# A hybrid S5 and attention layer on one core: TensorE's order written out by hand in the recurrence stage, the gelu in one activation, the skip folded into the kernel matrix

## The chip, the cores and the metric

The kernel runs on one core of one Trainium2 chip. The metric is the device time of one execution in microseconds; the median of several runs is compared. The profile names the engines PE (TensorE, matmuls), PEld (its weight loads), DVE (VectorE), ACT (ScalarE), POOL (GpSimd) and SP (SyncE, which here only issues transfers). Each engine works through its own instructions in a fixed order.

## What is computed

One encoder layer over two requests (1024 and 256 tokens, 1280 in all, model width 1024). After an RMS norm one projection gives eight parts. Branch A is a bidirectional diagonal state-space mixer, branch B differential attention. What the change touches is the mixer's recurrence:

```
bu = einsum('ngpc,lgc->nlgp', B_bar, us)
_, h_f = associative_scan(combine, (a[0], bu[0]))
_, h_b = associative_scan(combine, (a[1], bu[1]), reverse=True)
y = real(C[0] h_f + C[1] h_b)
y = y + d_skip * u
ys = gelu(y)                       # tanh form
ys = ys * sigmoid(ys @ w_glu + b_glu) * silu(zs)
...
ya = rmsnorm(diff_attention(rotary(q), rotary(k), v)) * silu(za)
merged = sigmoid(gs) * (ys @ wb[0]) + sigmoid(ga) * (ya @ wb[1])
out = rmsnorm(x + merged @ w_out)
```

## The kernel before

Everything is float32; large matmuls are made of three products of a high and a low part. Tokens are taken in steps of T = 8: J = 160 columns of eight tokens each (128 for the long request, 32 for the short). There are NG = 32 groups of 16 channels with 64 complex states in two directions.

The stages in order: norm, transposition and v; projections for xs, q and k, beside which a generator (`prep_gen`) computes the recurrence's tables, pair of groups by pair, into DRAM (`wb_d`, `wc_d`, `kt_d`, `tt_d`); the recurrence; attention; GLU, merge and output projection.

Four of the projection's parts (zs, za, gs, ga: 24 tiles of 128 columns) are wanted only at the end. They are the filler: `filler_gen` yields after each step of three matmuls (L637 to L639), eight steps for a chunk of columns, three chunks for a tile, 576 steps in all. A chunk is copied out by ACT (`zo`, L643); a tile's weights are loaded by ACT's queue, cast by ACT (L233) and their low part computed by POOL (L234). `fill(n)` traces n steps. In the kernel before the recurrence holds no fill calls: `fill(F_PRE * KD)` = 176 steps stand ahead of the attention's loops, 288 in them, the rest in the GLU stage. The framework's planner simulates the program and sets each engine's order by its own estimates, so the filler steps land in the recurrence where it finds PE free.

The recurrence goes over eight blocks of NB = 4 groups. For a block PE makes the in-projection `pr`, `pi` (L709, L710; weights `wb`, one buffer; moving operand `U`), DVE multiplies them by the table `tb` (L715 to L718), POOL adds and subtracts (L719, L720) to give `bm`, DVE runs four scans (L727, L728) with the decay `rt` that POOL makes (L703), zeroes borders (L731, L732) and turns the result back by `tb` into `e` (L737 to L742). PE makes the out-projection (L749 to L751) from `e` (weights `wcm`) and from `U` (weights `mt`, read from `kt_d`). DVE adds the skip (L754), ACT squares, DVE scales and multiplies (L759, L760), ACT takes a sigmoid (L761), DVE multiplies (L762): that is the gelu. `e` has one buffer; `tb`, `wcm`, `mt` and `U` have two. All loads go through SP (`U` L672, `mt` L675, `wb` L687, `tb` L688, `wcm` L689), in SP's order.

Of the kernel before, what the change touches and what calls it, by code (L numbers as in the profile page):

```python
# [11 lines left out]
F32 = mybir.dt.float32  # L12
F32R = mybir.dt.float32r
I32 = mybir.dt.int32
AF = mybir.ActivationFunctionType
ALU = mybir.AluOpType
# [12 lines left out]
J = JL + JS  # L29
# [6 lines left out]
LAM_INIT = 0.8 - 0.6 * math.exp(0.0)  # L36
CHUNKS = ((0, 512), (512, 512), (1024, 256))
MAGIC = 12582912.0
F_PRE = 22
F_LONG = (4, 1, 2, 0)  # L40
F_SHORT = (3, 2, 3, 0)
F_CHUNKS = ((0, 432), (432, 424), (856, 424))
# [75 lines left out]
def bc(ap, axis, n):  # L118
    shape = list(ap.shape)
    shape.insert(axis, n)  # L120
    return ap.unsqueeze(axis).broadcast_to(shape)
# [3 lines left out]
def kernel(  # L125
# [6 lines left out]
    V, G, A, PE, SP = nc.vector, nc.gpsimd, nc.scalar, nc.tensor, nc.sync  # L132
# [28 lines left out]
    ident = cp.tile([128, 128], F32, name="ident")  # L161
# [8 lines left out]
    r8 = cp.tile([128, NG], F32, name="r8")  # L170
    dcol = cp.tile([128, NG], F32, name="dcol")
    rmask = cp.tile([128, J], F32, name="rmask")
# [75 lines left out]
    def prep_gen():  # L248
# [18 lines left out]
        ps = tr_bank()  # L267
# [13 lines left out]
        t1, t2 = sc("t1"), sc("t2")  # L281
# [27 lines left out]
        for i, dst in enumerate((Cr, Ci)):  # L309
            ps = tr_bank()  # L310
# [74 lines left out]
        for pb in range(NPB):  # L385
# [8 lines left out]
            for n in range(2):  # L394
                for r in range(2):
                    A.activation(Bm[:, :, r, 32 * n:32 * n + 32], Bb[:, :, 16 * r:16 * r + 32], AF.Copy,
                                 scale=hmask[:, n:n + 1])
# [6 lines left out]
            ps = tr_bank()  # L404
            for r in range(2):
                for g in range(2):
                    o = (r * 2 + g) * 128
# [5 lines left out]
            wc = qq.tile([128, 2, 2, T, GC], F32, tag="wc", name="wc", bufs=2)  # L413
# [11 lines left out]
            ps = tr_bank()  # L425
            for g in range(2):
                o = ps[64 * g:64 * g + 64]
# [6 lines left out]
            kt = qq.tile([128, 144], F32, tag="kt", name="kt", bufs=2)  # L434
            A.copy(kt[:, 16:144], ps[:, 16:144])
            for g in range(2):
                A.copy(kt[64 * g:64 * g + 32, 0:16], ps[64 * g:64 * g + 32, 0:16])
            kv = kt_d[pb // 4]
            for g in range(2):
                gi = 2 * (pb % 4) + g  # L440
# [36 lines left out]
    with ExitStack() as p0:  # L477
# [53 lines left out]
        for i in range(10):  # L531
# [6 lines left out]
            ps = mm_bank()  # L538
# [113 lines left out]
    def fill(steps, ins=None):  # L652
        with after(ins):
            for _ in range(steps):
                next(filler, None)
# [4 lines left out]
    with ExitStack() as p2:  # L660
        sp_ = p2.enter_context(tc.tile_pool(name="s5", bufs=1, reuse_waits="tile"))
        ps_b = p2.enter_context(tc.tile_pool(name="ps_b", bufs=2, space=PSUM, reuse_waits="tile"))
        NB = 4
        NBLK = NG // NB
        U = {}
        M = {}
        Y = {}

        def load_u(q):
            u = sl.tile([128, 8, J], F32, tag="U", name="U", bufs=2)  # L670
            for t in range(T):
                SP.dma_start(u[t * 16:(t + 1) * 16], xs_d[q][t].rearrange("(g c) j -> c g j", c=GC))  # L672
            mt = sl.tile([128, 8, 128], F32, tag="mt", name="mt", bufs=2)
            for t in range(T):
                SP.dma_start(mt[t * 16:(t + 1) * 16],  # L675
                             kt_d[q][:, :, (7 - t) * 16:(7 - t) * 16 + 128].rearrange("g c w -> c g w"))
            M[q] = mt
            U[q] = u

        def load_blk(b):  # L680
            tb = sl.tile([128, 2, NB, J], F32, tag="tb", name="tb", bufs=2)
            wb = sl.tile([128, 2, NB, 128], F32, tag="wb", name="wb")
            wc = sl.tile([128, 2, NB, 128], F32, tag="wcm", name="wcm", bufs=2)
            for h in range(2):
                pb = 2 * b + h
                gsl = slice(2 * h, 2 * h + 2)
                SP.dma_start(wb[:, :, gsl], wb_d[pb])  # L687
                SP.dma_start(tb[:, :, gsl], tt_d[pb])  # L688
                SP.dma_start(wc[:, :, gsl], wc_d[pb])  # L689
            return tb, wb, wc  # L690

        load_u(0)
        blk = load_blk(0)
        for b in range(NBLK):
            q, gb = b // 2, (b % 2) * NB
            if b % 2 == 0:
                Y[q] = nrm.tile([128, 8, J], F32, tag="A", name="Y")
                if q + 1 < 4:
                    load_u(q + 1)
            tb, wb, wc = blk  # L700
            u, y, mt = U[q], Y[q], M[q]
            rt = sp_.tile([128, NB, J], F32, tag="rt", name="rt")
            G.tensor_tensor(rt, bc(rmask, 1, NB), bc(r8[:, b * NB:(b + 1) * NB], 2, J), op=ALU.mult)  # L703
            bm = sp_.tile([128, 2, NB, J], F32, tag="bm", name="bm", bufs=2)
            for h in range(NB // 2):
                pr_ = ps_b.tile([128, 2, J], F32, tag="pr", name="pr")
                pi_ = ps_b.tile([128, 2, J], F32, tag="pi", name="pi")
                for g in range(2):
                    PE.matmul(pr_[:, g], wb[:, 0, 2 * h + g], u[:, gb + 2 * h + g], start=True, stop=True)  # L709
                    PE.matmul(pi_[:, g], wb[:, 1, 2 * h + g], u[:, gb + 2 * h + g], start=True, stop=True)  # L710
                t1 = sp_.tile([128, 2, J], F32, tag="t1", name="t1")
                t2 = sp_.tile([128, 2, J], F32, tag="t2", name="t2")
                gsl = slice(2 * h, 2 * h + 2)
                tr_, ti_ = tb[:, 0, gsl], tb[:, 1, gsl]
                V.tensor_tensor(bm[:, 0, gsl], pr_, tr_, op=ALU.mult)  # L715
                V.tensor_tensor(t2, pr_, ti_, op=ALU.mult)
                V.tensor_tensor(t1, pi_, ti_, op=ALU.mult)
                V.tensor_tensor(bm[:, 1, gsl], pi_, tr_, op=ALU.mult)  # L718
                G.tensor_tensor(bm[:, 0, gsl], bm[:, 0, gsl], t1, op=ALU.add)  # L719
                G.tensor_tensor(bm[:, 1, gsl], bm[:, 1, gsl], t2, op=ALU.subtract)  # L720
            n = NB * J
            z = []
            for r in range(2):
                zz = sp_.tile([128, n + 2], F32, tag=f"z{r}", name=f"z{r}")
                rf = rt.rearrange("p g j -> p (g j)")
                bf = bm[:, r].rearrange("p g j -> p (g j)")
                V.tensor_tensor_scan(zz[0:64, 2:n + 2], rf[0:64], bf[0:64], 0.0, ALU.mult, ALU.add)  # L727
                V.tensor_tensor_scan(zz[64:128, 0:n][:, ::-1], rf[64:128, ::-1], bf[64:128, ::-1], 0.0,  # L728
                                     ALU.mult, ALU.add)
                zv = zz[:, 1:n + 1].rearrange("p (g j) -> p g j", j=J)  # L730
                V.memset(zv[0:64, :, 0:J:JL], 0.0)  # L731
                V.memset(zv[64:128, :, JL - 1:J:JS], 0.0)  # L732
                z.append(zv)
            e = sp_.tile([128, 2, NB, J], F32, tag="e", name="e")
            f1 = sp_.tile([128, NB, J], F32, tag="f1", name="f1")
            f2 = sp_.tile([128, NB, J], F32, tag="f2", name="f2")
            V.tensor_tensor(e[:, 0], z[0], tb[:, 0], op=ALU.mult)  # L737
            V.tensor_tensor(f1, z[1], tb[:, 1], op=ALU.mult)
            V.tensor_tensor(e[:, 0], e[:, 0], f1, op=ALU.subtract)
            V.tensor_tensor(e[:, 1], z[1], tb[:, 0], op=ALU.mult)  # L740
            V.tensor_tensor(f2, z[0], tb[:, 1], op=ALU.mult)
            V.tensor_tensor(e[:, 1], e[:, 1], f2, op=ALU.add)  # L742
            if b + 1 < NBLK:
                blk = load_blk(b + 1)
            for h in range(NB // 2):
                py = tr_bank()[:, :2 * J].rearrange("p (g j) -> p g j", j=J)
                for g in range(2):
                    gg = 2 * h + g
                    PE.matmul(py[:, g], wc[:, 0, gg], e[:, 0, gg], start=True, stop=False)  # L749
                    PE.matmul(py[:, g], wc[:, 1, gg], e[:, 1, gg], start=False, stop=False)  # L750
                    PE.matmul(py[:, g], mt[:, gb + gg], u[:, gb + gg], start=False, stop=True)  # L751
                for g in range(2):
                    gg = 2 * h + g
                    V.scalar_tensor_tensor(y[:, gb + gg], u[:, gb + gg], dcol[:, b * NB + gg:b * NB + gg + 1],  # L754
                                           py[:, g], op0=ALU.mult, op1=ALU.add)
            g1 = nrm.tile([128, NB, J], F32, tag="B", name="g1")
            yb = y[:, gb:gb + NB]
            A.activation(g1, yb, AF.Square)
            V.tensor_scalar(g1, g1, 0.044715, 1.0, op0=ALU.mult, op1=ALU.add)  # L759
            V.tensor_tensor(g1, g1, yb, op=ALU.mult)  # L760
            sig = A.activation(g1, g1, AF.Sigmoid, scale=2.0 * math.sqrt(2.0 / math.pi))  # L761
            V.tensor_tensor(yb, yb, g1, op=ALU.mult)  # L762
            if b % 2 == 1:
                for t in range(T):
                    SP.dma_start(gy_d[q][t].rearrange("(g c) j -> c g j", c=GC), y[t * 16:(t + 1) * 16])

    with tc.issue_after(sig.ins):
        tables = A.preload_act_table_set("natural_log_exp_and_others")
# [381 lines left out]
```

## Time and profile before

| what | value |
|---|---|
| median of 3 runs | 1159.61 us (1158.87 to 1161.73) |
| profiled execution | 1156.2 us, its span 1154.0 us |
| granted TensorE clock, mean | 0.982 |
| busy: PE, DVE, ACT, POOL | 94%, 71%, 40%, 34% |

The span runs from the first to the last instruction; the execution's own time has a little around it. Matmuls overlap, so PE's busy time counts stretches in which any is under way, and the distance between two starts is what a matmul costs. The granted clock is a share of full speed.

### The profile page before, as it was taken

The numbers are of one execution on the slowest core, as the hardware profiler recorded it, in microseconds if no ns is written. First come the engines' busy times: TensorE is split into PE (matmuls) and PEld (weight loads), VectorE is DVE, ScalarE is ACT, GpSimd is POOL, SyncE is SP. The second block draws the span as 40 slices with busy tenths as digits, with TensorE's granted clock in tenths as the row PEclk, the third lists the DMA queues.
The fourth block names the chain that finished last, engine by engine and source line by source line (L and its number), as shares of the span: only waits on it lengthen the run. The fifth ranks groups of instructions, "written<-read, shape, count | busy, mean of one in ns | idle before, by whom it ended". The sixth has DMA issues, their size and how long they took to land.

```text
span 1154.0 us, 18198 instructions
## 1 busy us (share of the span) xinstructions
PE 1086.1 (94%) x6539; PEld 998.3 (87%) x6539; DVE 817.4 (71%) x1482; ACT 457.0 (40%) x911; POOL 396.9 (34%) x559
## 2 busy tenths in 40 slices
PE   5999999999989788889999999999999999999997
PEld 5887788778888787779998999889999999998997
DVE  5857968987549999977687687597353575666524
ACT  4443332132211111155565565465364454554322
POOL 1499989831134334212122122121133002520032
PEclk9998999999999888999999999999999999999999
DMA  7834453554475666661641733531455985469222
GB/s 225 228 102 151 144 176 113 184 187 139 158 201 188 149 163 174 174 158 57 158 126 49 197 96 89 152 96 43 124 177 175 283 243 140 136 177 283 70 56 93
DMA packets 193786, 174.13 MB, mean 151 GB/s; under 512 B 33568, under 2 KB 166688, under 8 KB 193696
## 3 DMA queue, kind: packets, MB, share of 16 engines
q1 hardware_dynamic: 158368, 144.65, 43.6%
q10 hardware_dynamic: 35328, 28.32, 7.7%
q8 instruction: 52, 0.85, 0.3%
q14 instruction: 38, 0.31, 0.1%
HBM read 114.23 MB, written 58.69 MB: 150 GB/s over the span
## 4 chain that ended last, share of the span: by engine, by line
PE 51%; DVE 20%; DMA 11%; POOL 8%; issue 6%; ACT 3%; SPq 2%; POOLq 0%; DVEq 0%; ACTq 0%
PE mm L637 6%; PE mm L638 6%; PE mm L639 6%; PE mm L240 3%; PE mm L241 3%; PE mm L242 3%; PE tr L1090 2%; DVE mx L827 2%; PE tr L1092 2%; PE tr L1091 2%; PE S L823 2%; DMA wqs<-in_w_out_dram 2%; DMA wst<-in_w_in_dram 2%; PE S L825 2%; PE tr L848 2%
## 5 line engine op out<-in xcount | busy, mean ns | idle before, releaser
L637 PE MATMUL mm<-hTh,wh 128*128 128x424 f32 (+1 forms) x576 | 210.1, 365 | 1.6 <-ACT zo L643 1.6
L639 PE MATMUL mm<-hTh,wl 128*128 128x424 f32 (+1 forms) x576 | 206.2, 358 | 0.0
L638 PE MATMUL mm<-hTl,wh 128*128 128x424 f32 (+1 forms) x576 | 206.0, 358 | 0.0
L838 POOL TENSOR_SCALAR p<-p,rs 128x1024 f32<-128x1024 f32 (+1 forms) x40 | 41.3, 1034 | 234.0 <-DVE rs L836 154.9
L637 PEld LDWEIGHTS mm<-hTh,wh 128*128 128x128 f32 x576 | 108.6, 189 | 6.6 <-ACT zo L643 2.4
L638 PEld LDWEIGHTS mm<-hTl,wh 128*128 128x128 f32 x576 | 108.8, 189 | 4.3 <-issue 0.2
L639 PEld LDWEIGHTS mm<-hTh,wl 128*128 128x128 f32 x576 | 108.8, 189 | 3.2
L827 DVE TENSOR_REDUCE mx<-S 128x1 f32<-128x1024 f32 (+1 forms) x80 | 84.3, 1058 | 36.9 <-PE S L825 36.1
L240 PE MATMUL mm<-hTh,wh 128*128 128x512 f32 (+1 forms) x288 | 105.8, 367 | 3.6 <-DVE m L604 1.8
L241 PE MATMUL mm<-hTl,wh 128*128 128x512 f32 (+1 forms) x288 | 104.4, 362 | 0.0
L242 PE MATMUL mm<-hTh,wl 128*128 128x512 f32 (+1 forms) x288 | 103.6, 360 | 0.0
L234 POOL TENSOR_TENSOR wl<-wst,wh 128x1024 fp32r<-128x1024 f32 x24 | 62.1, 2588 | 114.0 <-ACT wh L233 114.0
L831 ACT ACTIVATE p<-S,mx 128x1024 f32<-128x1024 f32 (+1 forms) x80 | 79.2, 992 | 53.8 <-DVE mx L828 53.2
L1090 PE MATMUL tr<-wqh,mh 128*128 128x256 f32 x320 | 89.8, 281 | 1.9 <-DVE o L1094 1.8
L1091 PE MATMUL tr<-wql,mh 128*128 128x256 f32 x320 | 89.2, 279 | 0.0
L1092 PE MATMUL tr<-wqh,ml 128*128 128x256 f32 x320 | 89.0, 279 | 0.0
L240 PEld LDWEIGHTS mm<-hTh,wh 128*128 128x128 f32 x288 | 54.7, 190 | 14.5 <-ACT xo L571 2.3
L1097 POOL TENSOR_TENSOR o<-o,finB 128x256 f32<-128x256 f32 x30 | 28.7, 960 | 102.5 <-ACT jk L1096 102.5
L1090 PEld LDWEIGHTS tr<-wqh,mh 128*128 128x128 f32 x320 | 60.1, 188 | 2.9 <-DVE o L1094 2.9
L241 PEld LDWEIGHTS mm<-hTl,wh 128*128 128x128 f32 x288 | 54.7, 190 | 9.2 <-issue 1.4
L242 PEld LDWEIGHTS mm<-hTh,wl 128*128 128x128 f32 x288 | 54.7, 190 | 8.3
L1091 PEld LDWEIGHTS tr<-wql,mh 128*128 128x128 f32 x320 | 60.2, 188 | 0.0
(397 smaller groups left out, 2888.7 us busy)
## 6 DMA issues: line engine op xcount, KB each, us to landing
wst<-in_w_in_dram ACTq DMA_DIRECT2D x24, 512.0 KB, 4.3
wst<-in_w_in_dram SPq DMA_DIRECT2D x16, 512.0 KB, 5.8
wst<-in_w_branch_dram SPq DMA_DIRECT2D x32, 256.0 KB, 4.5
wqs<-in_w_out_dram SPq DMA_DIRECT2D x16, 512.0 KB, 4.4
tt_d<-tt SPq DMA_DIRECT2D x16, 320.0 KB, 2.2
tb<-tt_d SPq DMA_DIRECT2D x16, 320.0 KB, 5.0
zt<-gs_d SPq DMA_DIRECT2D x16, 320.0 KB, 4.2
x<-in_x_sample_dram SPq DMA_DIRECT2D x8, 512.0 KB, 5.3
```

The source lines that it names most:

```text
L234: e.tensor_tensor(l, st, h, op=ALU.subtract)
L240: PE.matmul(ps[:, :n], wh[:, k, :], hTh[:, k, c0:c0 + n], start=(k == 0), stop=False)
L241: PE.matmul(ps[:, :n], wh[:, k, :], hTl[:, k, c0:c0 + n], start=False, stop=False)
L242: PE.matmul(ps[:, :n], wl[:, k, :], hTh[:, k, c0:c0 + n], start=False, stop=(k == KD - 1))
L637: PE.matmul(ps[:, :n], wh[:, k, :], hTh[:, k, c0:c0 + n], start=(k == 0), stop=False)
L638: PE.matmul(ps[:, :n], wh[:, k, :], hTl[:, k, c0:c0 + n], start=False, stop=False)
L639: PE.matmul(ps[:, :n], wl[:, k, :], hTh[:, k, c0:c0 + n], start=False, stop=(k == KD - 1))
L827: V.tensor_reduce(mx, S[:, :nk], axis=AX.X, op=ALU.max)
L831: A.activation(p[:, :nk], S[:, :nk], AF.Exp, bias=mx, scale=1.0 / math.sqrt(HD), accum_out=sm[:, t:t + 1])
L1090: PE.matmul(ps[:, :256], mh[:, k, ts_], oh_[:, k], start=(k == 0), stop=False)
L1091: PE.matmul(ps[:, :256], mh[:, k, ts_], ol_[:, k], start=False, stop=False)
L1092: PE.matmul(ps[:, :256], ml[:, k, ts_], oh_[:, k], start=False, stop=(k == 7))
```

## The change

- In the recurrence stage PE's instructions keep the order in which they are written (`tc.manual_schedule`). That order is: `fill(36)`, in-projection of block 0, and then for each block b the in-projection of block b + 1, `fill(13)`, the out-projection of b, `fill(4)`. That is 172 filler steps; the 176 ahead of the attention go (`F_PRE = 0`).
- The loop is cut into `in_mm`, `scan` and `out_mm`. Block b + 1's `wb`, `tb`, `wcm` are requested before the next `U`, and `mt` is loaded by a function of its own after them.
- `e` has two buffers.
- `rt` is made by four ACT copies of 160 columns with a scale instead of one POOL multiply of 640.
- The gelu is one ACT activation (`Gelu_apprx_tanh`) straight from PSUM, two groups at a time.
- The skip is added to the diagonal of the lag-0 block of `kt` during preparation (two small DVE instructions a pair of groups, in place of two ACT copies), so that the product of `mt` and `U` contains it.
- Two of DVE's four multiplies of the in-projection change places.

```diff
-F_PRE = 22
+F_PRE = 0
+S_PRE, S_MID, S_END = 36, 13, 4
...
             for g in range(2):
-                A.copy(kt[64 * g:64 * g + 32, 0:16], ps[64 * g:64 * g + 32, 0:16])
+                o = slice(64 * g, 64 * g + 16)
+                V.scalar_tensor_tensor(kt[o, 0:16], ident[o, 64 * g:64 * g + 16], dcol[o, 2 * pb + g:2 * pb + g + 1],
+                                       ps[o, 0:16], op0=ALU.mult, op1=ALU.add)
...
+        def load_m(q):
             mt = sl.tile([128, 8, 128], F32, tag="mt", name="mt", bufs=2)
...
-            G.tensor_tensor(rt, bc(rmask, 1, NB), bc(r8[:, b * NB:(b + 1) * NB], 2, J), op=ALU.mult)
+            for g in range(NB):
+                A.activation(rt[:, g], rmask, AF.Copy, scale=r8[:, b * NB + g:b * NB + g + 1])
...
                 V.tensor_tensor(bm[:, 0, gsl], pr_, tr_, op=ALU.mult)
+                V.tensor_tensor(t1, pi_, ti_, op=ALU.mult)
                 V.tensor_tensor(t2, pr_, ti_, op=ALU.mult)
-                V.tensor_tensor(t1, pi_, ti_, op=ALU.mult)
...
-            e = sp_.tile([128, 2, NB, J], F32, tag="e", name="e")
+            e = sp_.tile([128, 2, NB, J], F32, tag="e", name="e", bufs=2)
...
-                for g in range(2):
-                    gg = 2 * h + g
-                    V.scalar_tensor_tensor(y[:, gb + gg], u[:, gb + gg], dcol[:, b * NB + gg:b * NB + gg + 1],
-                                           py[:, g], op0=ALU.mult, op1=ALU.add)
-            g1 = nrm.tile([128, NB, J], F32, tag="B", name="g1")
-            yb = y[:, gb:gb + NB]
-            A.activation(g1, yb, AF.Square)
-            V.tensor_scalar(g1, g1, 0.044715, 1.0, op0=ALU.mult, op1=ALU.add)
-            V.tensor_tensor(g1, g1, yb, op=ALU.mult)
-            sig = A.activation(g1, g1, AF.Sigmoid, scale=2.0 * math.sqrt(2.0 / math.pi))
-            V.tensor_tensor(yb, yb, g1, op=ALU.mult)
+                act = A.activation(y[:, gb + 2 * h:gb + 2 * h + 2], py, AF.Gelu_apprx_tanh)
...
+        load_u(0)
+        blks = {0: load_blk(0)}
+        load_m(0)
+        with tc.manual_schedule(engines={mybir.EngineType.PE}):
+            fill(S_PRE)
+            cur = in_mm(0, blks[0])
+            for b in range(NBLK):
+                if b + 1 < NBLK:
+                    blks[b + 1] = load_blk(b + 1)
+                if b % 2 == 0 and b // 2 + 1 < 4:
+                    load_u(b // 2 + 1)
+                    load_m(b // 2 + 1)
+                e = scan(b, blks[b], *cur)
+                if b + 1 < NBLK:
+                    cur = in_mm(b + 1, blks[b + 1])
+                fill(S_MID)
+                sig = out_mm(b, blks.pop(b), e)
+                fill(S_END)
```

## Rows read from the trace of the kernel before

**Rows 1.** The page: busy time and share of the span of each engine.

```profile
PE 1086.1 (94%) x6539; PEld 998.3 (87%) x6539; DVE 817.4 (71%) x1482; ACT 457.0 (40%) x911; POOL 396.9 (34%) x559
```

**Rows 2.** Windows, recurrence and attention: us, busy of each engine, clock, DMA.

```profile
331.00:503.00 172.00, 142.80 (x748) 134.33 (x747) 163.95 (x234) 27.13 (x41) 60.32 (x45) 0.91 0.64 173
503.00:820.00 317.00, 311.94 (x1840) 289.67 (x1839) 233.76 (x428) 177.26 (x356) 70.44 (x52) 1.00 0.36 104
```

**Rows 3.** Waits of PE, 331 to 503 us: total, times, longest.

```profile
PE tr L749 <- DVE e L739: 8.8, 4, 5.3
PE pr L709 <- DMA wb<-wb_d: 8.7, 3, 4.4
PE tr L749 <- DVE Y L754: 8.3, 3, 4.7
```

**Rows 4.** Timeline of PE: start, duration, instruction.

```profile
304.31 0.36 PE L637 MATMUL mm<-hTh,wh 128*128 128x432 f32 x1
...
306.05 0.36 PE L637 MATMUL mm<-hTh,wh 128*128 128x432 f32 x1
...
348.51 0.56 PE L637 MATMUL mm<-hTh,wh 128*128 128x424 f32 x1
...
357.13 0.43 PE L750 MATMUL tr<-e,wcm 128*128 128x160 f32 x2
...
359.84 0.43 PE L709 MATMUL pr<-U,wb 128*128 128x160 f32 x2
```

**Rows 5.** Groups by line, PE, 304 to 503 us: count, busy, mean, idle before.

```profile
L637 PE MATMUL mm<-hTh,wh 128*128 128x424 f32 (+1 forms) x183 | 66.4, 363 | 1.6 <-ACT zo L643 1.6
```

**Rows 6.** Groups by line, DVE, 332 to 492.6 us (until the last e).

```profile
L754 DVE SCALAR_TENSOR_TENSOR Y<-U,dcol,tr 128x160 f32<-128x160 f32 x25 | 8.1, 374 | 0.4 <-DMA gy_d<-Y 0.3
L762 DVE TENSOR_TENSOR Y<-Y,g 128x640 f32<-128x640 f32 x6 | 7.2, 1199 | 0.1
L759 DVE TENSOR_SCALAR g<-g 128x640 f32<-128x640 f32 x6 | 5.8, 972 | 0.0
L760 DVE TENSOR_TENSOR g<-g,Y 128x640 f32<-128x640 f32 x6 | 5.5, 916 | 0.1
```

**Rows 7.** Timeline of DVE: first multiply, an rt's neighbours, last e.

```profile
332.10 0.49 DVE L715 TENSOR_TENSOR bm<-pr,tb 128x320 f32<-128x320 f32 x1 [22.07 <-PE pr L709]
...
346.07 1.53 DVE L737 TENSOR_TENSOR e<-z,tb 128x640 f32<-128x640 f32 x1
347.53 0.81 DVE L741 TENSOR_TENSOR f<-z,tb 128x640 f32<-128x640 f32 x1
...
491.86 0.81 DVE L742 TENSOR_TENSOR e<-e,f 128x640 f32<-128x640 f32 x1
```

**Rows 8.** Groups by line, POOL, 304 to 503 us.

```profile
L234 POOL TENSOR_TENSOR wl<-wst,wh 128x1024 fp32r<-128x1024 f32 x8 | 23.2, 2902 | 44.9 <-ACT wh L233 44.9
...
L703 POOL TENSOR_TENSOR rt<-rmask,r 128x640 f32<-128x640 f32 x8 | 10.0, 1255 | 35.7 <-DVE z L731 23.3 <-DVE z L732 6.3 <-DVE z L728 3.7
```

**Rows 9.** Timeline of SP's queue: transfers issued, start and time to issue.

```profile
318.17 4.10 SPq L675 DMA_DIRECT2D mt<-kt_d  x8
...
324.23 0.62 SPq L687 DMA_DIRECT2D wb<-wb_d  x1
...
408.73 1.19 SPq L689 DMA_DIRECT2D wcm<-wc_d  x2
...
411.33 1.29 SPq L687 DMA_DIRECT2D wb<-wb_d  x2
```

**Rows 10.** DMA issues, 320 to 352 us: count, size, median us to landing.

```profile
wb<-wb_d SPq DMA_DIRECT2D x4, 256.0 KB, 5.6
```

**Rows 11.** Groups by line, ACT, 304 to 503 us.

```profile
L758 ACT ACTIVATE g<-Y 128x640 f32<-128x640 f32 x8 | 5.9, 739 | 58.4 <-DVE Y L754 58.4
```

**Rows 12.** A one-column DVE instruction (attention), and the busiest window of preparation.

```profile
L828 DVE TENSOR_SCALAR mx<-mx 128x1 f32<-128x1 f32 x79 | 11.4, 145 | 0.4
...
200.00:250.00 50.00, 46.85 (x250) 36.89 (x249) 47.31 (x85) 10.58 (x31) 32.76 (x46) 1.00 0.56 185
```

More of the change, by code (lines that the diff above doesn't have):

```diff
@@ L672, in load_u @@
                 SP.dma_start(u[t * 16:(t + 1) * 16], xs_d[q][t].rearrange("(g c) j -> c g j", c=GC))
+            U[q] = u
+        def load_m(q):
             mt = sl.tile([128, 8, 128], F32, tag="mt", name="mt", bufs=2)
@@ L677, in load_u @@
             M[q] = mt
-            U[q] = u
         def load_blk(b):
@@ L690, in load_blk, with in_mm @@
             return tb, wb, wc
-        load_u(0)
-        blk = load_blk(0)
-        for b in range(NBLK):
+        def in_mm(b, blk):
             q, gb = b // 2, (b % 2) * NB
[L696 to L699, printed above, removed]
             tb, wb, wc = blk
-            u, y, mt = U[q], Y[q], M[q]
+            u = U[q]
             rt = sp_.tile([128, NB, J], F32, tag="rt", name="rt")
-            G.tensor_tensor(rt, bc(rmask, 1, NB), bc(r8[:, b * NB:(b + 1) * NB], 2, J), op=ALU.mult)
+            for g in range(NB):
+                A.activation(rt[:, g], rmask, AF.Copy, scale=r8[:, b * NB + g:b * NB + g + 1])
             bm = sp_.tile([128, 2, NB, J], F32, tag="bm", name="bm", bufs=2)
@@ L720, with scan @@
                 G.tensor_tensor(bm[:, 1, gsl], bm[:, 1, gsl], t2, op=ALU.subtract)
+            return rt, bm
+        def scan(b, blk, rt, bm):
+            tb = blk[0]
             n = NB * J
@@ L742, with out_mm @@
             V.tensor_tensor(e[:, 1], e[:, 1], f2, op=ALU.add)
-            if b + 1 < NBLK:
-                blk = load_blk(b + 1)
+            return e
+        def out_mm(b, blk, e):
+            q, gb = b // 2, (b % 2) * NB
+            wc = blk[2]
+            u, mt = U[q], M[q]
+            if b % 2 == 0:
+                Y[q] = nrm.tile([128, 8, J], F32, tag="A", name="Y")
+            y = Y[q]
             for h in range(NB // 2):
@@ L765 @@
                     SP.dma_start(gy_d[q][t].rearrange("(g c) j -> c g j", c=GC), y[t * 16:(t + 1) * 16])
+            return act
+        load_u(0)
[16 more added lines that the diff above has]
+                fill(S_END)
     with tc.issue_after(sig.ins):
```

## The prediction, on record before the changed kernel was run

> **What bounds the kernel now.** I read the busy shares first. TensorE (PE) is busy 94% of the span [rows 1], so only time in which PE idles or runs at its lower clock can be won. The windows by stage say where that is [rows 2]: in the attention (503 to 820 us) PE is busy 312 of 317 us at clock 1.00, so little is lost there. The recurrence (331 to 503) has PE at 143 of 172 us and a granted clock of 0.91, while VectorE (DVE) is busy 164 of 172.
>
> PE's waits in that stage name DVE twice, 8.8 us for e and 8.3 us for Y, and a load of wb for 8.7 us [rows 3]. So the stage goes at DVE's pace.
>
> How much PE loses there: in the filler (gate projection) nine matmuls start within 1.74 us, 0.193 us each [rows 4], so a step of three is 0.58 us. Twenty passes of the recurrence's matmuls fill 357.13 to 359.84, 0.1355 us each, and its in-projection, 16 passes, takes 2.2 us a block; the 24 passes of the out-projection make 3.25 us, together 43.4 us in eight blocks. From 304 to 503 PE started 183 steps [rows 5], 106.1 us. With 43.4, about 2 us of leftover preparation matmuls, and 1.9 us of eight score matmuls it had 153.4 us of work in 199: **45.6 us are lost**. That is all that the change can win in this stage.
>
> **The change, part by part.**
>
> *DVE loses four kinds of work.* Y's multiply-add (skip), the gelu's scalar step and its two multiplies go: 8.1, 5.8, 5.5 and 7.2 us of the time until the last e [rows 6], 26.6 us in 43 instructions. Consecutive ones overlap by 0.07 us (an instruction that begins at 346.07 and lasts 1.53 ends at 347.60, and the next begins at 347.53 [rows 7]), so 26.6 - 3.0 = 23.6, say 24 us. DVE works from 332.10 to 492.67, 160.5 us, almost without a gap.
>
> *rt leaves POOL for ScalarE.* Eight instructions, 10.0 us of POOL [rows 8]. Where one meets an e multiply, at 346.07, that lasts 1.53 instead of 0.81 us [rows 7]; over the seven inside the stage the stretches add to 3.7 us, 1.7 of them on instructions that go anyway. I count 2 us. The Trainium skill, SBUF — State Buffer, Who interferes with whom, says that a DVE instruction with two SBUF inputs and a GpSimd one that reads SBUF shut each other out for a whole instruction; taken for every rt that would be 10 us, and the sum below 8 us lower. The row at 346.07 agrees with the shutting out, but most rts here meet a DVE instruction with an input in PSUM or none.
>
> *What comes back.* The removed scalar step averages 0.97 us and the last multiply 1.20 [rows 6], against about 0.5 and 0.8 undisturbed: part of their time was POOL's weight split (eight of 2.9 us [rows 8]) or its bm adds standing in the way, and these will now meet other instructions. I give back 3 us. DVE then needs 160.5 - 24 - 2 + 3 = **137.5 us** from first multiply to last e. Bounds: below, the undisturbed times of what stays (eight multiplies at 0.40, four scans at 1.5, memsets 0.45, six e instructions at 0.74 make 14.1 a block, 112.5 in all); above, another 1 us a block for the wait on POOL's last bm add, which gelu work used to cover: 145.5.
>
> *The start.* SP issues U, then eight mt loads for 4.1 us, then block 0's tables, the second half of wb at 324.23 [rows 9]. With mt behind, that half issues at about 320.1 and, with 0.6 us to issue and 5.6 to land [rows 10], is there at 326.3. In the hand order PE has 36 steps first: 304.3 + 20.9 + 2 of preparation = 327.2. So the in-projection starts at 327.2 instead of 331.1 and DVE at about 328. mt is due at the first out-projection, some 15 us later; its loads hide behind the first scans.
>
> *The second block.* There is one wb buffer, so block 1's wb issues when in-projection 0 is over (329.4); its second half is fourth on SP (1.9 us) and lands at 336.9. PE, in order, idles 7.5 us there. DVE is at block 0's scans and does not notice; PE later catches up.
>
> *The end of the stage.* Last e at 328 + 137.5 = 465.5, out-projection 3.3 more: about 469, against 498. PE by then has done 36 + 8 x 13 + 7 x 4 = 168 steps, 97.4 us, with 43.4 and 2 us: 142.8 of 165 us. Lost: 22.2. The steps that were not done here run later, on a PE that has no idle time there; they are inside the balance. **Gain 45.6 - 22.2 = 23.4 us.**
>
> *The second e tile* lets e of a block be written while PE still reads the one before; DVE never waited for it, so nothing is counted. *Gelu in one activation*: two of 320 columns in place of two of 640 at 0.74 us [rows 11]; ScalarE (busy 27 of 172 us) has room for them and for rt's 32 copies (between 0.3 and 0.7 us each, 10 to 22 us).
>
> *The skip in the preparation.* 32 small DVE instructions (16 x 16, out of PSUM) take the place of ScalarE copies. Nearest rows: 0.145 us for one column, 0.374 for the same operation on 160 [rows 6, 12]; 16 columns lie near the first, so 5 us of DVE (bounds 4.6 and 12). DVE is at 47 of 50 us in the tightest part of that stage [rows 12] but has 10 to 30% free elsewhere. I charge 3 us, bounds 0 and 9.
>
> **Sum.** The profiled execution took 1156.2 us: 1156.2 - 23.4 + 3 = 1135.8. The median of the runs is 3.4 us above it, so **1139 us**.
>
> **Rivals.**
>
> *PE's own order sets the pace.* From 339 us (in-projection 1 done) the hand order needs 7.5 + 3.25 + 2.3 + 2.2 = 15.25 us a block: six such, then 13.05 and 10.75, ends at 454.3. That needs DVE to do its part in 123 us, within its bounds but only if most POOL stretches vanish. Lost 7.5, gain 38.1, and with 3 for the preparation 1124 us. For it: PE's stretch is arithmetic. Against: in all windows POOL's wl and bm do stretch DVE.
>
> *rt gives back all of its time.* If each of the eight rts held DVE up for its whole 1.25 us, DVE's part is 8 us shorter, 129.5, and the time 1131 us. For it: the row at 346.07; against: the six others, most of which cost DVE under 1 us. This is what the SBUF page named above would make of it.
>
> *ScalarE becomes the wait.* rt must be ready before each scan, and queues behind zo copies and gelus that wait for PE. If it stands behind the previous gelu: 3.25 us of out-projection, the gelu, 1.5 us of copies, less the 3.2 us of multiplies that run meanwhile, over 2 us a block: stage end near 484, 1154 us.
>
> *The wb load holds up PE (slower).* With one wb buffer and one SP queue the order of issues decides. In the trace wcm goes out at 408.73 and wb only at 411.33 [rows 9], tb between them, and wcm's buffer has to wait for an out-projection. Here that would be four issues ahead of wb and two of its own, 3.7 us, and landing 4.1, against 2.3 us of filler: a stall of 5.5 us a block, and some 1.7 more because PE comes back slow (after the wait for wb that ends at 346 a filler matmul takes 0.56 us, not 0.36 [rows 4], and it goes on like that for 4 us). Six blocks: 43 us on the 454.3, lost 50.7, time 1156.2 + 5.1 + 3 + 3.4 = 1168 us. It decides from 5.9 us a block upward. Against: wb comes free at the in-projection, well before wcm, and SP's order in most blocks had wb first.
>
> **Chances.** DVE's pace as summed 0.50; rt's whole time 0.10; PE's order 0.20; ScalarE 0.07; nothing left after a dearer preparation 0.04; wb 0.09. A difference under 0.3% cannot be told from none here. Faster 0.86, same 0.05, slower 0.09. The range goes from PE's order with a free preparation (1121) to the upper bounds of DVE (gain 15.4) and preparation (9): 1156.2 - 15.4 + 9 + 3.4 = 1153, and the ScalarE case beside it: 1120 to 1154.
>
> **What would show it.** In the changed profile: first bm multiply near 328; last e near 465; DVE busy above 90% between; PE's wait for e in most blocks, under 2 us each; a gap of some 7 us ahead of the second in-projection; clock above 0.95. A wait of DVE for rt, or PE waiting for wb in every block, would say that a rival holds. The number fails most easily in DVE's 137.5 us, whose stretches by POOL depend on who meets whom, and in later stages, if an order there shifts.

## The result, and the profile after

The changed kernel takes 1165.05 us (median of 9 runs, 1161.31 to 1169.93) against 1159.53 us for the kernel before (9 runs beside it): a ratio of 1.0055 [1.0039, 1.0071], 0.6% slower. 1139 was forecast. Its profiled execution took 1166.0 us, its span 1164.2, 10.2 more than before.

Where the 10.2 us come from, by three marks that both traces have (the start of the last matmul of the last out-projection, the start of the last transposition of an attention unit, the end of the span):

| stretch | before | after | difference | of it moved filler steps | left |
|---|---|---|---|---|---|
| start to last out-projection | 498.2 | 479.9 | -18.3 | -8 steps, -4.6 | -13.7 |
| to last transposition (attention) | 324.6 | 348.1 | +23.5 | +4 steps, +2.3 | +21.2 |
| to the end (GLU, merge, output) | 331.2 | 336.2 | +5.0 | +4 steps, +2.3 | +2.7 |

So the recurrence gained, though less than the forecast 20.4 us (23.4 less the 3 charged for the preparation, which lies in the same stretch), and the attention, in whose code the diff changes nothing, lost more. The page's first line (answers to [rows 1]) and the windows of recurrence and attention (us, busy of PE, PEld, DVE, ACT, POOL with instructions, clock, DMA share, GB/s; answer to [rows 2]):

```profile
PE 1082.7 (93%) x6539; PEld 997.9 (86%) x6539; DVE 783.6 (67%) x1458; ACT 456.6 (39%) x911; POOL 377.9 (32%) x551
```

```profile
327.00:480.00 153.00, 126.53 (x713) 123.61 (x712) 128.87 (x176) 30.70 (x67) 43.45 (x38) 0.91 0.69 185
480.00:828.20 348.20, 330.09 (x1896) 305.64 (x1895) 236.96 (x429) 178.11 (x359) 71.07 (x53) 0.98 0.35 101
```

The recurrence still has PE idle for 26.5 of 153 us at the clock of before, 0.91. In the attention, where PE had idled 5 of 317 us at clock 1.00, it now idles 18 of 348 at 0.98.

PE's waits up to the last out-projection (answer to [rows 3]; total, times, longest):

```profile
PE pr L709 <- DMA wb<-wb_d: 11.1, 1, 11.1
PE pr L709 <- DVE z L735: 9.4, 1, 9.4
PE pr L709 <- DVE e L746: 6.0, 1, 6.0
```

All three stand ahead of an in-projection, and by SP's queue all three are waits for `wb`. Two rows name DVE, as what ended last before PE went on; but an in-projection reads no z and no e, and `wb` was issued only at 332.26 and 432.34, and takes 3.0 to 6.6 us to land in this stage. The first of the three in time is the gap forecast ahead of the second block (PE's timeline: start, duration, instruction, idle before):

```profile
328.17 0.43 PE L710 MATMUL pi<-U,wb 128*128 128x160 f32 x2
338.00 0.87 PE L709 MATMUL pr<-U,wb 128*128 128x160 f32 x2 [9.40 <-DVE z L735]
```

The longest is seen on SP's queue (start, time to issue; answer to [rows 9]). The one buffer of `wb` was free when the in-projection before ended, at 373.2, and the program requests `wb` before the next `U`. But SP's order is the planner's, and in it `wb` goes out behind `tb`, which had to wait for block 2's e, behind `wcm`, and then behind 13 us of stores and loads; the last 3 us before it SP waited. The same happens again at 432.34.

```profile
375.17 1.17 SPq L693 DMA_DIRECT2D tb<-tt_d  x2
376.44 1.22 SPq L694 DMA_DIRECT2D wcm<-wc_d  x2
377.76 4.97 SPq L766 DMA_DIRECT2D gy_d<-Y  x8
382.83 3.79 SPq L675 DMA_DIRECT2D U<-xs_d  x8
386.67 4.32 SPq L681 DMA_DIRECT2D mt<-kt_d  x8
394.10 1.18 SPq L692 DMA_DIRECT2D wb<-wb_d  x2
```

DVE, for its part, now waits for PE. Its waits from 327 us, and its first multiply and last e (answer to [rows 7]):

```profile
DVE bm L715 <- PE pr L709: 25.9, 6, 15.9
DVE z L731 <- POOL bm L719: 2.4, 8, 0.3
```

```profile
327.28 0.49 DVE L715 TENSOR_TENSOR bm<-pr,tb 128x320 f32<-128x320 f32 x1 [15.88 <-PE pr L709]
...
472.08 0.82 DVE L746 TENSOR_TENSOR e<-e,f 128x640 f32<-128x640 f32 x1
```

The 15.9 us lie before the first multiply; 10.0 are in the stage. The last out-projection starts 3.9 us after that e has ended (476.82 against 472.90): PE, behind by then, still had the 17 steps that the written order puts between the last two out-projections, 9.8 us.

The attention's new idle time, PE's waits from 480 us on:

```profile
PE tr L869 <- ACT sqh L892: 7.1, 4, 3.1
PE S L844 <- ACT p L852: 3.2, 3, 2.7
PE S L844 <- DMA gs_d<-zo: 1.9, 1, 1.9
PE mm L640 <- ACT zo L646: 1.7, 2, 1.2
PE tr L869 <- DVE mx L849: 1.6, 2, 1.1
```

Four of the five name ACT or DVE, which are busy only 51% and 68% of the stretch: they had the time, but not at that place of their order. Not all of the loss is idle time: between the two marks PE's busy time grew too, from 319.5 to 330.0 us, 2.3 of it for the four steps, at a clock of 0.98 in place of 1.00.

### The profile page after: what moved, and what is told of

Same layout as the page of the kernel before. It is cut to its first block, busy times and chain, and to the rows that moved or that the text cites. A ratio compares the mean times of both kernels' runs of the same rounds, so it can differ in the third digit from the quotient of the medians.

```text
span 1164.2 us, 18199 instructions
## 1 busy us (share of the span) xinstructions
PE 1082.7 (93%) x6539; PEld 997.9 (86%) x6539; DVE 783.6 (67%) x1458; ACT 456.6 (39%) x911; POOL 377.9 (32%) x551
## 4 chain that ended last, share of the span: by engine, by line
PE 55%; DVE 17%; DMA 11%; POOL 7%; issue 5%; ACT 3%; SPq 2%; POOLq 0%; ACTq 0%; DVEq 0%
PE mm L640 6%; PE mm L641 6%; PE mm L642 6%; PE xb L979 3%; PE xb L980 3%; DMA wst<-in_w_in_dram 3%; PE xb L978 3%; PE mm L241 3%; PE mm L242 3%; PE mm L243 3%; PE tr L1111 2%; PE tr L1112 2%; PE tr L1113 2%; PE S L844 2%; PE S L846 2%
## 5 line engine op out<-in xcount | busy, mean ns | idle before, releaser
L640 PE MATMUL mm<-hTh,wh 128*128 128x424 f32 (+1 forms) x576 | 213.3, 370 | 1.7 <-ACT zo L646 1.7
L235 POOL TENSOR_TENSOR wl<-wst,wh 128x1024 fp32r<-128x1024 f32 x24 | 58.4, 2432 | 150.1 <-ACT wh L234 149.8
L646 ACT COPY zo<-mm 128x424 f32<-128x424 f32 (+1 forms) x72 | 36.9, 513 | 95.1 <-PE mm L642 82.8
```

The source lines that it names most:

```text
L235: e.tensor_tensor(l, st, h, op=ALU.subtract)
L640: PE.matmul(ps[:, :n], wh[:, k, :], hTh[:, k, c0:c0 + n], start=(k == 0), stop=False)
```

## The experiments

All times are medians against runs of the kernel before on the same chip. "Attention" is the time from the last out-projection to the last transposition of a unit, "steps ahead" the filler steps traced ahead of the attention's loops. Steps added directly ahead of the loops (e6, e7, e10 and the pairs below) run inside that stretch, 2.3 us for each four.

**Where the filler enters the attention.** One number is changed in each: 40 in place of 36 steps ahead of the first in-projection; four steps fewer in the kernel *before*; 4, 8 or 12 more steps directly ahead of the attention.

```diff
# e1_phase176
-S_PRE, S_MID, S_END = 36, 13, 4
+S_PRE, S_MID, S_END = 40, 13, 4
# e2_before172 (the kernel before)
-        fill(F_PRE * KD)
+        fill(F_PRE * KD - 4)
# e7_plus4 (e6_plus8: 8, e10_plus12: 12)
-        fill(F_PRE * KD)
+        fill(4)
```

> The changed kernel with 40 instead of 36 filler steps ahead of the first in-projection: 176 in the stage, as many as stood ahead of the attention before, so a chunk of eight steps ends where the stage ends. Theory A (the attention lost its 20 us because 172 steps leave the filler in the middle of a chunk, so its copies and weight casts fall at other points of each attention unit): the stretch from the last out-projection to the attention's last transposition goes from 348.6 us back to about 325, and the time to about 1145 us. Theory B (the planner's order of the attention is simply drawn anew whenever something ahead of it moves): the stretch lies anywhere between 320 and 355 us, with no relation to the phase. Both: the recurrence ends about 2 us later than 479.6.

> The kernel before with 172 instead of 176 filler steps ahead of the attention; nothing else is changed. Theory A (phase of the filler): the attention gets 15 to 20 us longer and the time goes to about 1175 us. Theory B (order drawn anew): the attention changes by some us in either direction, the time stays within 1150 to 1170 us with no rule in it. The recurrence should be as before, last out-projection at 498 us give or take 3.

> The changed kernel, hand order and 172 steps in the stage as they are, with 8 more steps ahead of the attention's loops: 180 in all, a whole chunk more, so the same place within a chunk of 8 (4) but another within a tile of 24 (12, was 4). Theory A1 (what counts is where chunks end in a unit): the attention stays long, near 348 us less nothing, time about 1165 us. Theory A2 (what counts is where a tile's weight cast and split fall, just ahead of the short request's units at 172 and 4 us behind them at 176): the cast moves by 8 steps, away from that place, and the attention shortens by 10 us or more. Theory N (the number of steps done early counts, not the place): it shortens, 180 being more than 176.

> The changed kernel with 4 more steps ahead of the attention's loops: 176 in all, the recurrence and its hand order exactly as they were. Theory A (place of the filler within chunk or tile): the attention takes about 325 us plus the 2.3 us of the four steps, and the time is about 1145 to 1150 us, as with 40 steps ahead of the first in-projection. If what helped there was the later start of the in-projections, nothing moves and it stays near 1165 us.

> The changed kernel with 12 more steps ahead of the attention's loops: 184 in all, at a chunk's end (0 of 8) but at 16 of 24 within a tile. Theory A1 (chunk): as good as with 176, attention about 325 us plus 7 us for the twelve steps, time about 1146 to 1150 us. Theory A2 (weight cast): it depends on where the cast falls now, and can be as long as with 172. Theory N (number): as good as with 176 or better.

| kernel | steps ahead | time, ratio [95%] | attention | ACT's wait for a chunk's end |
|---|---|---|---|---|
| before | 176 | 1159.5 | 324.6 | 6.7 |
| e2 | 172 | 1184.62, 1.0213 [1.0196, 1.023] | 348.7 | 26.5 |
| after | 172 | 1165.05, 1.0055 | 348.1 | 25.4 |
| e1 | 176 | 1148.80, 0.9908 [0.9893, 0.9922] | 326.8 | 6.2 |
| e7 | 176 | 1147.84, 0.9913 [0.9897, 0.9928] | 329.9 | 8.5 |
| e6 | 180 | 1175.85, 1.0161 [1.013, 1.0193] | 359.3 | 28.9 |
| e10 | 184 | 1166.55, 1.0061 [1.0039, 1.0083] | 348.8 | 29.8 |

Four steps more make the changed kernel 16 or 17 us faster (e1, e7), and four fewer make the kernel before 25 us slower. So the attention's loss belongs to the number of steps ahead of it and to nothing else in the change: the kernel before, unchanged but for this, loses as much (348.7 and 348.1 us). It is no matter of fewer or more (172, 180 and 184 are all bad), nor of whole chunks (184 is 23 chunks of eight). The last column, from ACT's waits, goes along with the loss in every one of these rows:

```profile
ACT zo L646 <- PE mm L642: 25.4, 13, 3.4
```

that is the changed kernel (with its copies, exps and casts queued behind), and with four steps more:

```profile
ACT zo L646 <- PE mm L642: 8.5, 9, 2.9
```

**The weights in the attention.** From tile 9 on a tile uses the weights of an earlier one: no load, no cast on ACT, no split on POOL. Once with 172 and once with 176 steps.

```diff
-                if ci == 0 and i + 2 < len(tiles):
+                if ci == 0 and i + 2 >= 9:
+                    ws.append((wh, wl))
+                elif ci == 0 and i + 2 < len(tiles):
```

> The changed kernel (172 steps), in which the filler loads, casts and splits no weights from tile 9 on and multiplies by those of tiles 7 and 8 again; so 15 of the 24 gate tiles come out of wrong weights. All matmuls, copy-outs and waits for banks are kept. Theory A2 (the attention's length depends on where the weight cast and split fall against the units): with neither, the attention takes about 325 us or less, whatever the place, as in the same run with 176. Theory A1 (what falls badly are the chunks' copy-outs): it stays 15 us or more above the run with 176.

> The same, no weights loaded, cast or split from tile 9 on (15 of 24 gate tiles out of wrong weights), with 4 more steps ahead of the attention: 176. Theory A2: within 6 us of the run with 172, near 320 us for the attention. Theory A1: 15 us or more shorter than with 172.

1168.22 and 1149.23 us (one run each), attention 349.9 and 333.6. The difference of 16 to 19 us stays, so loads, casts and splits do not make it. ACT waits 43.6 and 24.6 us for chunk ends here, so that column marks the worse of a pair and is no measure of the loss.

**The order in the recurrence.** The planner's order in place of the written one (e3; e5 with 176 steps); `wb` loaded by ACT's queue (e4); two `wb` buffers on top of e7 (e8); `rt` made by POOL again on top of e5 (e13).

```diff
# e3_planner, e5_planner176 (S_PRE = 40 too)
-        with tc.manual_schedule(engines={mybir.EngineType.PE}):
+        with ExitStack():
# e4_wb_act
-                SP.dma_start(wb[:, :, gsl], wb_d[pb])
+                A.dma_start(wb[:, :, gsl], wb_d[pb])
# e8_wb2 (with fill(4))
-            wb = sl.tile([128, 2, NB, 128], F32, tag="wb", name="wb")
+            wb = sp_.tile([128, 2, NB, 128], F32, tag="wb", name="wb", bufs=2)
# e13_rt_pool (with e5's edits)
-            for g in range(NB):
-                A.activation(rt[:, g], rmask, AF.Copy, scale=r8[:, b * NB + g:b * NB + g + 1])
+            G.tensor_tensor(rt, bc(rmask, 1, NB), bc(r8[:, b * NB:(b + 1) * NB], 2, J), op=ALU.mult)
```

> The changed kernel with the hand-set order taken away: the planner orders TensorE in the recurrence from the same 172 steps. If the DVE work that was removed made the stage shorter, its last out-projection stays within 5 us of 479.6 or comes earlier, since the planner can place filler ahead of a late in-projection; if the hand order made it, it goes back toward 498. Theory A: the attention stays near 348 us; theory B: it is drawn anew, 320 to 355 us.

> The changed kernel with the loads of wb issued from ScalarE's queue instead of SP's, where they stood behind tb, the stores of Y, U and mt. Theory C (those three late in-projections, 27 us of TensorE waits, cost the stage the 10 us that it missed of the prediction): TensorE's waits ahead of the in-projections fall under 8 us, DVE has no gap at 390 and 435 us, and the last out-projection comes at about 468 instead of 479.6. Rival (ScalarE's in-order queue holds the loads up just as long, or DVE's own pace was the limit): it stays within 3 us of 479.6. The total follows only if the attention keeps its 348.6 us.

> The changed kernel with 40 steps ahead (176 in the stage) and without the hand-set order: the two single findings together. If they add (176 steps gave the attention about 21 us, the planner's order in place of the hand's gave the recurrence about 12), the last out-projection comes near 470 us, the attention takes about 326 us from there, and the time is 1133 to 1138 us, 2% below the kernel before. If one of them only hides the other, it stays at 1146 to 1150 us.

> The changed kernel with the hand-set order and 172 steps in the stage, four more ahead of the attention (176 in all, as in the run with plus 4), and two buffers for wb in place of one. Theory C (the late in-projections come from wb's load, which with one buffer is issued behind the stores of Y and the loads of tb, U and mt): a block's wb is requested a block earlier, TensorE's waits ahead of the in-projections fall from 27 us to under 8, the last out-projection comes near 468 instead of 479.6 and the time near 1137 us. Rival (it is the hand order's own place of the in-projection, ahead of 13 steps, or DVE's pace, that ends the stage): within 3 us of 479.6 and of 1148 us.

> The planner's order with 176 steps in the stage (1136.8 us), with rt made by POOL again as in the kernel before. By the prediction's sum rt's move is worth 2 us of DVE (bounds 0 and 10): last out-projection 475 to 476 instead of 473.6, time about 1139 us. By the rule that shuts DVE out for all of rt's time it is 8 to 10 us: 1145 us. If rt on ScalarE had cost something (rival: its copies behind other work), it gets faster.

| kernel | steps ahead | time, ratio [95%] | last out-projection | attention |
|---|---|---|---|---|
| after | 172 | 1165.05 | 479.9 | 348.1 |
| e3 | 172 | 1153.36, 0.9951 [0.9936, 0.9966] | 467.9 | 345.1 |
| e4 | 172 | 1158.81, 1.0002 [0.9978, 1.0026] | 478.3 | 346.4 |
| e8 | 176 | 1141.28, 0.9853 [0.9834, 0.9871] | 475.2 | 328.9 |
| e5 | 176 | **1136.82, 0.9809 [0.9788, 0.983]** | 473.6 | 327.0 |
| e13 | 176 | 1143.66, 0.9869 [0.9849, 0.9889] | 479.9 | 327.4 |

The written order costs 12 us (after against e3, e1 against e5), most or all of it in the recurrence (12.0 and 8.6 us of the traces' 13.3 and 7.5). With the planner's order DVE has no wait for an in-projection left inside the stage of e5, and its stretch from first multiply to last e is 136.2 us in e3 and 135.7 in e5: there the stage does go at DVE's pace. The stalls for `wb` are about half of the 12 us: a second buffer brings 6.6 us (e7 to e8), and the waits of e8 are no longer mostly for it:

```profile
PE tr L760 <- DVE e L743: 7.2, 1, 7.2
PE pr L709 <- DMA wb<-wb_d: 6.1, 2, 4.9
PE pr L709 <- DMA mt<-kt_d: 4.4, 1, 4.4
```

Another queue alone (e4) moves the stage by 1.6 us. The load is late there too: the in-projection before ends at 376.6, but `wb` goes out on ACT's queue at 385.95, in an idle time of ACT of 8.6 us that the profile puts down to a store of `gy_d`; the next time it is 12.1 us. Why ACT's queue waits there is not shown. The whole kernel gets 6.2 us faster, but its ten runs spread from 1153.6 to 1170.0 us, and only those 1.6 us lie in the stage.

The windows from 303 us to the last out-projection, e5 first and e13, with `rt` on POOL, second:

```profile
303.00:473.80 170.80, 157.18 (x884) 149.40 (x884) 138.03 (x195) 36.73 (x81) 51.48 (x40) 0.97 0.73 200
```

```profile
303.00:480.10 177.10, 162.16 (x896) 153.75 (x895) 145.58 (x197) 27.81 (x49) 61.32 (x48) 0.95 0.72 193
```

With eight POOL instructions more DVE is busy 7.5 us longer with two instructions more, and the time is 6.8 us longer. The rows show where: in seven of the eight blocks `rt` on POOL meets the first e multiply, which takes 1.53 us or more there and 0.83 without (the same instruction in e5, then in e13):

```profile
L741 DVE TENSOR_TENSOR e<-z,tb 128x640 f32<-128x640 f32 x8 | 6.6, 826 | 0.3
L740 DVE TENSOR_TENSOR e<-z,tb 128x640 f32<-128x640 f32 x8 | 11.8, 1481 | 0.3
```

**The order in the attention.** TensorE's order there as the program writes it (e14, e15); the same with each unit's filler in one piece behind the transpositions (e16, e17); a chunk's copy-out held until the fourth step of the next chunk (e18); each filler step held until the one before it (e20).

```diff
# e14_hand172, e16_rhythm172; e15_hand176, e17_rhythm176 with fill(4)
+        with tc.manual_schedule(engines={mybir.EngineType.PE}):
             for h in range(NH):
...
# e16 and e17 too
-F_LONG = (4, 1, 2, 0)
-F_SHORT = (3, 2, 3, 0)
+F_LONG = (0, 0, 7, 0)
+F_SHORT = (0, 0, 8, 0)
# e18_late_copy172
...
+                    if k == LATE and late:
+                        with after(last):
+                            late.pop()()
...
# e20_in_turn172
-                    PE.matmul(ps[:, :n], wh[:, k, :], hTh[:, k, c0:c0 + n], start=(k == 0), stop=False)
+                    with after(last):
+                        PE.matmul(ps[:, :n], wh[:, k, :], hTh[:, k, c0:c0 + n], start=(k == 0), stop=False)
```

> The changed kernel with TensorE's order in the attention kept as the program writes it (172 filler steps ahead of it, as in the changed kernel). Left open so far: with 172 or 180 steps ahead the attention takes 15 to 20 us more than with 176, and TensorE's orders there differ between these kernels far beyond a shift of four steps. Theory O, the order that the planner chose for 172 steps is what costs: with one written order the attention must take the same with 172 and 176 steps, within 5 us (4 steps are 2.3 us of it), however long that is. Theory P, the place of the chunk ends in the units costs by itself: this kernel's attention is then 15 to 20 us longer than that of the same with 176.

> The kernel with the written order in the attention and four more filler steps ahead of it (176). Theory O: attention (last out-projection to last transposition of a unit) within 5 us of the one with 172, times within 5 us. Theory P: 15 to 20 us shorter.

> The changed kernel with TensorE's order in the attention written out as the trace of the 176-step kernels mostly shows it: both score products of a unit, eight transpositions of the one before, then seven filler steps (eight in short units) and the output product. 172 steps ahead. Theory O: the attention takes 325 to 332 us, as in the 176-step kernels, the time is about 1146 us, and the same with four steps more. Theory P: 345 us or more here, the time about 1165.

> The same written order with 176 steps ahead. Theory O: attention and time within 5 us of those with 172 steps. Theory P: 15 to 20 us shorter than with 172.

> The changed kernel, 172 filler steps ahead of the attention; the only edit: ScalarE's copy-out of a finished filler chunk may be issued only after the fourth step of the next chunk (PSUM has a second bank for it), so that ScalarE's queue holds no copy-out that waits for a filler matmul still to run. The waits of ScalarE for the last filler matmul of a chunk sum to 25.4 us in the attention of the changed kernel (22 to 30 in all loaded kernels with 172, 180 or 184 steps) and to 5.5 to 8.5 in those with 176. Theory Z, these waits hold up the copies and exps behind them in ScalarE's order, and TensorE with them: with the slack they fall under 10 us, the attention takes 325 to 335 us and the kernel about 1150 us. Rival, the waits are only a sign of the planner's other order, which costs by itself: the waits fall but the attention stays above 342 us and the time at 1160 or more.

> The changed kernel, 172 filler steps ahead of the attention; the only edit: a filler step may be issued only after the step before it. In the trace of the changed kernel the planner runs the steps of two chunks through one another (six steps of a 432-column chunk, four of the next, then two of the first; five, seven, one, seven, and so on), so that a chunk is left one to five steps short while the next one runs. That is also why the late copy-out changed nothing: the fourth step of the next chunk came before the last of this one. With 176 steps the planner does it as well, at other places. Theory I, the order that the planner falls into with 172 steps, units and filler through one another, is what costs: in turn, each chunk's eight steps run together, ScalarE waits for a chunk's end less than 15 us in all, the attention takes 325 to 335 us and the time is 1143 to 1153 us. Rival, 172 is a bad place for the chunk ends however the planner orders the steps: attention 342 us or more, time 1160 or more.

| kernel | steps ahead | time, ratio [95%] | attention | ACT's wait for a chunk's end |
|---|---|---|---|---|
| e14 | 172 | 1173.47, 1.0145 [1.0114, 1.0177] | 354.9 | 30.6 |
| e15 | 176 | 1183.53, 1.0208 [1.018, 1.0236] | 363.4 | 29.6 |
| e16 | 172 | 1198.77, 1.0362 [1.0327, 1.0397] | 378.7 | 8.4 |
| e17 | 176 | 1216.14, 1.0501 [1.0485, 1.0516] | 392.6 | 20.9 |
| e18 | 172 | 1162.26, 1.0042 [1.0022, 1.0062] | 345.5 | 25.4 |
| e20 | 172 | 1155.06, 0.9978 [0.996, 0.9996] | 335.7 | 11.6 |

Both theories put ahead of the first four fell. With a written order 176 steps are not better: the attention is 8 and 14 us longer, the time 10 and 17, so 176 is no good place by itself; and the difference is over 5 us, so an order that is the same does not make the place indifferent. Both written orders are slower than the planner's. In e16 ACT waits only 8.4 us for chunk ends, and yet the attention takes 378.7 us; the transpositions alone wait 29.7 us for DVE:

```profile
PE tr L869 <- DVE p L860: 29.7, 17, 2.3
```

e18 tested nothing: ACT waited 25.4 us as before, since the edit had no slack to give. The filler's rows in the changed kernel tell the likely reason (PE's timeline, the first matmul each time the chunk changes):

```profile
612.30 0.44 PE L640 MATMUL mm<-hTh,wh 128*128 128x432 f32 x1
...
616.36 0.44 PE L640 MATMUL mm<-hTh,wh 128*128 128x424 f32 x1
...
622.85 0.44 PE L640 MATMUL mm<-hTh,wh 128*128 128x432 f32 x1
...
629.56 0.43 PE L640 MATMUL mm<-hTh,wh 128*128 128x424 f32 x1
```

Those four stretches hold three, six, five and seven steps, where a chunk has eight: the planner runs the steps of neighbouring chunks through one another. It does so with 176 steps too, at other places. In e20 it cannot; the widths then come in whole chunks, eight and twice eight, and with the same 172 steps the attention gets 12.4 us shorter (PE idle 12.7 instead of 18.1 us, clock 1.00):

```profile
476.90:812.60 335.70, 322.99 (x1895) 301.00 (x1894) 229.11 (x429) 176.41 (x360) 70.48 (x53) 1.00 0.36 105
```

The time falls by 10.0 us. That is just outside what was expected of theory I (335.7 against 325 to 335 us, 1155.1 against 1143 to 1153), and short of the rival's 342 and 1160. With 176 steps in the planner's own order PE idles less still, 4.5 us (e1):

```profile
482.40:809.20 326.80, 322.25 (x1895) 299.50 (x1894) 235.45 (x429) 178.63 (x359) 70.13 (x52) 1.00 0.37 109
```

Of the 12.4 us, 5.4 are idle time and 7.1 busy time, at a clock of 1.00 in place of 0.98. So at the same number of steps another order is worth 12 us, set beside the 21 lost. The same edit with 176 steps was not run, so what it would bring there is not known. That the order does it through ACT's wait, one way that it could, is argued and not shown: in one stall of the changed kernel PE's transposition waits 2.88 us for a square that ACT runs only after 5.13 us of waiting for the store of `ya`, with no chunk in it.

```profile
633.25 1.11 PE L869 MATMUL tr<-ident,p 128*128 128x128 f32 x4 [2.88 <-ACT sqh L892]
```

```profile
632.54 0.37 ACT L891 COPY ya<-tr 128x256 f32<-128x256 f32 x1 [5.13 <-DMA ya_d<-ya]
```

The other 9 us are nearly all idle time of PE (12.7 us in e20, 4.5 in e1); what makes it idle there stays open.

## Why the prediction was wrong

**The step that failed** is the sentence that the steps not done here "run later, on a PE that has no idle time there; they are inside the balance". It counted the steps' own time and took the attention as it was. The attention's order is the planner's and depends on how many steps have gone before. Four fewer moved it from one with 4.5 to 5 us of idle PE to one with 18, and cost 21.2 us; the same four fewer cost the kernel before 25 us (e2). Put back, they give a faster kernel: 1147.84 us. "In later stages, if an order there shifts", the prediction named as a way to fail, but it had no place in the range nor a chance.

**The gain in the recurrence** was summed at 23.4 us, 20.4 with the preparation, and came to 13.7. Of its terms:
- *DVE's 137.5 us.* First multiply to last e is 145.6 us (327.28 to 472.90), 10.0 of it waiting for in-projections. Without them 135.6: the term was right within 2 us, though partly by luck, since `rt` brought some 5 us more than was counted and the rest that much less, to within those 2 us. It was not the limit.
- *The start* was forecast at 327.2 and came at 326.3; the preparation charged with 3 us cost nothing that shows.
- *The second block's gap* was 9.4 us for 7.5.
- *The wb load.* The mechanism of the slower rival is real, but in two blocks, not six: 11.1 and 6.0 us. SP had `tb` and `wcm` ahead of `wb`, as the rival had it, and then also the stores of `gy_d` and the next `U` and `mt`, which it had not: 13 us more. The text argued against it that SP's order "in most blocks had wb first"; two blocks were enough. This and the second gap put PE behind its own written order, DVE behind PE, and left 4 us at the end: 480.2 in place of 469.
- *Who decides.* So the stage did not go at DVE's pace, as summed, but at PE's written order with its stalls, which was a rival at 0.20 without them. With the planner's order DVE's pace decides and the stage ends at 467.9 (e3), beside the 469 forecast.
- *`rt`* was taken at 2 us, from the stretches beside it in the kernel before. The text held that most `rt`s there met a DVE instruction with an input in PSUM or none; six of the seven in the stage overlapped one with both inputs in SBUF (L737 once, L741 twice, L762 three times). And with the gelu gone they meet others: in e13 the first e multiply, at 0.7 us or more each. The price is 6.8 us of the time and 7.5 of DVE's busy time (e13 against e5), near the 8 us by which the rival "`rt` gives back all of its time" moved the sum. The Trainium skill, SBUF — State Buffer, Who interferes with whom, calls the port pair that DVE and GpSimd share an exclusive lock, for which a DVE instruction with two SBUF inputs contends with a GpSimd one that reads SBUF; by that, an estimate for the eight instructions is at most their whole 10 us. The trace agrees with the lock: in e13 an e multiply that starts during an `rt` ends 0.7 us after that `rt`, about the 0.74 us that it takes by itself.

**The other rivals.** ScalarE did not become the wait: no PE wait in the recurrence names its gelu or `rt`, 32 copies of 0.417 us. The e5 kernel takes 1136.8 us, beside the 1139 forecast for the change. It is another kernel, so this does not confirm the sum term by term; but what the change removes was worth about what was summed, and the order it wrote (12 us) and the place where it left the filler (17 us) took it back. (In DVE's lower bound eight blocks of 14.1 us are 112.8, not 112.5; nothing hangs on it.)

## What to carry to other kernels

Where a planner orders a later stage, work moved across that stage's border is a change of its own: vary the amount by a few steps, in the old kernel too, before judging the rest of an edit; here four steps of 0.58 us were worth 16 to 25 us. An order written out for one engine must hold the transfers it waits for as well: with one buffer and one queue it met three waits of 6 to 11 us and came out 12 us behind the planner's order, and a second buffer gave 6.6 us back. When a stage gains and the kernel does not, compare the stretches between a few marks that both traces have, first of all those that the diff does not touch.

## What the runs showed of the hardware

PE came back slowly from each long wait. After the 9.4 us ahead of the second in-projection a matmul of 0.43 us took 0.87. The granted clock was at its lower level then, 1.2 GHz (0.50), while PE worked without a gap from 338.00 to 342.6, and after that at the upper one, 2.4 GHz (1.00):

```profile
338.00:342.60 4.60, 4.60 (x17) 4.60 (x18) 4.39 (x11) 1.27 (x4) 0.00 (x0) 0.50 0.77 136
342.70:348.00 5.30, 5.30 (x29) 5.16 (x29) 5.11 (x8) 0.51 (x1) 4.00 (x4) 1.00 0.80 205
```

Behind the waits of 11.1 and 6.0 us it was 0.50 as well (397.40 to 400.70, and 435.90 to 441.00).

What POOL costs DVE depends on which DVE instruction it meets, so it has to be read from the kernel after a change as well as from the one before: eight `rt`s of 1.25 us stretched what would stay by 2 us before the change, by the prediction's count, and cost 7.5 us of DVE's busy time in e13.
